# Three changes of order, and the second FFN matmul's right-hand loads issued by GpSimd, in a two-layer encoder kernel

## The chip, the cores and the metric

One core of a Trainium2 chip. The metric is the time of one execution in microseconds of device time (lower is better). Engines are named as in the profile: PE is TensorE, DVE is VectorE, ACT is ScalarE, POOL is GpSimd, and SP (SyncE) issues the transfers.

## The reference

A trunk of two encoder layers on x of 1024 tokens by 1024 features, all float32, conditioned by a vector c. Layer 0 mixes tokens with differential attention (8 heads, two score maps each), layer 1 with grouped-query attention (8 query heads, 2 key and value heads, RMS-normalised q and k, axial rotary). The feed-forward width is 2816.

```python
mod = (silu(c) @ ada_w[i] + ada_b[i])            # shift1, scale1, gate1, shift2, scale2, gate2
h = rmsnorm(x, norm1_g[i]) * (1.0 + scale1) + shift1
x = x + gate1 * mixer_i(h)                       # diff_attention or axial_gqa
h = rmsnorm(x, norm2_g[i]) * (1.0 + scale2) + shift2
gate, up = split(h @ w_in)
x = x + gate2 * ((silu(gate) * up) @ w_out)
...
return rmsnorm(x, final_g)
```

## The kernel before, in words

Activations are held transposed: 8 tiles `d` of 128 features, in two column chunks `c` of 512 tokens. Every float32 operand of a product is split into a high part (`whi`, a cast on ACT, L97) and a low part (`wlo`, a subtraction on DVE or POOL, L98), and one product becomes three matmuls: high times high (L107), high times low (L108), low times high (L109). One such "product of 128 by 512" is therefore three PE rows.

The framework orders each engine's instructions before the run, by the order in which they are written, by priorities, and by a simulated timeline. `issue_after(ins)` adds that an instruction comes behind `ins` on the same engine. Each engine then works its list in order, and so do the queues on which SP (and after the change POOL) issues transfers: a transfer that waits for its buffer holds up those behind it.

**Start (`start`, L344 to L420).** Row tiles of x are loaded (`load_x`, L360), eight of 128 by 1024. `scale` (L364) squares a tile on ACT, gets 1/rms by a power on POOL, and scales the tile in place (L372: chunk 0 on DVE, chunk 1 on POOL). `norm` (L374) transposes it on PE in blocks of 128 by 128 (L378), four to a bank, and ACT copies each bank out (L380). `mod(d)` (L382) loads two tiles of the modulation weights (L386), and DVE reduces them to the scale and shift of feature tile d (L387 to L390). `use(d, c)` (L393) makes the modulated h: the high part on ACT (L397), the same value on POOL (L398), the low part on DVE (L399); then come the products of tile d with the first head's q, k and v weights, 9 PE rows for each (d, c), 144 in all. The low parts of these three weights are made on POOL (`self.wlo`, L407).

**Layer 1, first projections (L684 to L709).** `steps` projects k, q or v of one head; a part is two of the eight feature tiles, so a projection of one chunk is four parts or 24 PE rows. `flush` (L622) finishes the k and q that are pending: a row sum on PE (L189), a power on POOL (L635), the rotary on DVE and POOL (L232 to L236), a broadcast of 1/rms on PE for k (L196) and its product on DVE (L643), then the split. Attention's first scores (L765 to L767) need k of both chunks.

**FFN input norm (`norm_parts`, L780).** For chunk 1, `step1` makes e, f and e - f for four pairs and writes the operands 7 and 3; `step2` subtracts three more times for each pair (`sub`, L797) and writes the operands 5, 6 and 4. The first products of chunk 1 (`plain(f, 1)`) take 3, 7, 7 and 3. All these subtractions and low parts are DVE's.

**Second FFN matmul (L1043 to L1166).** Seven products of blocks (a seven-product scheme in place of eight) in the order 1, 2, 6, 7, 5, 4, 3, each of 11 steps of 12 matmuls. A step needs one right-hand tile, loaded from the scratch `gd` into which the first matmul stored it (`right`, L1084; 77 loads a layer, 256 KB each, into `h` slots for products 1 and 2 and into eight `g` slots after that), and left-hand tiles of `w_out` (`left`, L1052; none to three a step, into five `raw` buffers and 22 `hb`). `ahead` writes a step's loads and splits LOOK = 4 steps ahead. At the end of products 2, 4, 5 and 3 POOL adds up squares for the next norm (`norm_acc`, L185).

Of the kernel before, what the change touches and what calls it, by code (L numbers as in the profile page):

```python
# [9 lines left out]
F32 = mybir.dt.float32  # L10
F32R = mybir.dt.float32r
AF = mybir.ActivationFunctionType
ALU = mybir.AluOpType
AX = mybir.AxisListType

P = 128
S = 1024
D = 1024
KT = 8
# [20 lines left out]
PARTS = 4  # L40
# [20 lines left out]
class Trunk:  # L61
# [33 lines left out]

    def split(self, hi, lo, src, eng=None):
        self.nc.scalar.copy(out=hi, in_=src)  # L97
        (eng or self.nc.vector).tensor_tensor(out=lo, in0=src, in1=hi.bitcast(F32), op=ALU.subtract)  # L98

    def mm3(self, ps, w, xs, n, w0=0, first=True, last=True, more=False):  # L100

# [242 lines left out]
    def start(self):  # L344

        nc, a = self.nc, self.a
        m, av = self.mods[0], self.avec[0][0]
        hs = [[None] * KT, [None] * KT]
        S0, S1 = self.t(self.pss, "S"), self.t(self.pss, "S")
        accs = [[S0[:, :CH], S0[:, CH:]], [S1[:, :CH], S1[:, CH:]], [self.bank("T"), self.bank("M")]]  # L350
        with self.tc.tile_pool(name="st", bufs=2) as st, self.tc.tile_pool(name="stx", bufs=8) as stx, \
                self.tc.tile_pool(name="stw", bufs=1) as stw, \
                self.tc.tile_pool(name="sta", bufs=4) as sta:
            xs = [[None] * KT, [None] * KT]

            def load_x(c):
                rows = []
                for i in range(4 * c, 4 * c + 4):
                    x = self.t(stx, "x0")
                    nc.sync.dma_start(out=x, in_=a["x"][i * P:(i + 1) * P, :])  # L360
                    rows.append(x)
                return rows

            def scale(c, rows):  # L364
                for x in rows:
                    sq = self.t(st, "sq")
                    r = self.t(st, "r0", [P, 2])
                    nc.scalar.activation(out=sq, in_=x, func=AF.Square, accum_out=r[:, 0:1])
                    nc.vector.tensor_scalar(out=r[:, 0:1], in0=r[:, 0:1], scalar1=1.0 / D, scalar2=EPS, op0=ALU.mult, op1=ALU.add)
                    nc.gpsimd.tensor_tensor(out=r[:, 1:2], in0=r[:, 0:1], in1=self.nhalf[:, :1], op=ALU.pow)  # L370
                    e = nc.vector if c == 0 else nc.gpsimd
                    e.tensor_scalar(out=x, in0=x, scalar1=r[:, 1:2], scalar2=0.0, op0=ALU.mult, op1=ALU.add)  # L372

            def norm(c, rows):  # L374
                for d in range(KT):
                    ps = self.bank("AT"[d % 2])
                    for i in range(4):
                        nc.tensor.transpose(ps[:, i * P:(i + 1) * P], rows[i][:, d * P:(d + 1) * P], self.ident)  # L378
                    xs[c][d] = self.hslot(F32)
                    nc.scalar.copy(out=xs[c][d], in_=ps)  # L380

            def mod(d):  # L382
                ds_ = slice(d, d + 1)
                for j in (1, 0):
                    w = self.t(sta, "aq")
                    nc.sync.dma_start(out=w, in_=a["ada_s"][j, d])  # L386
                    nc.vector.scalar_tensor_tensor(out=w, in0=w, scalar=1.0, in1=self.condr, op0=ALU.mult, op1=ALU.mult, accum_out=m[j][:, ds_])  # L387
                    b = C_ADAB + j * 8 + d
                    nc.vector.tensor_tensor(out=m[j][:, ds_], in0=m[j][:, ds_], in1=self.sm[:, b:b + 1], op=ALU.add)
                    if j == 1:  # L390
                        self.make_a(av[:, ds_], self.sm[:, C_N1 + d:C_N1 + d + 1], m[1][:, ds_])

            def use(d, c):  # L393
                sa, sb = av[:, d:d + 1], m[0][:, d:d + 1]
                hi, lo = hs[c][d] = self.hpair()
                h = self.t(st, "nh", [P, CH])
                nc.scalar.activation(out=hi, in_=xs[c][d], func=AF.Identity, bias=sb, scale=sa)  # L397
                nc.gpsimd.tensor_scalar(out=h, in0=xs[c][d], scalar1=sa, scalar2=sb, op0=ALU.mult, op1=ALU.add)  # L398
                nc.vector.tensor_tensor(out=lo, in0=h, in1=hi.bitcast(F32), op=ALU.subtract)  # L399
                for i in range(3):  # L400
                    self.mm3(accs[i][c], ws[i], hs[c][d:d + 1], 1, w0=d, first=d == 0, last=d == KT - 1)

            rows = [load_x(0), load_x(1)]
            self.condr = self.cond_row(self.cpool)
            mod(0)
            ws = []
            self.wlo = nc.gpsimd  # L407
            for i in range(3):
                raw = self.t(stw, "w0r") if i == 0 else None
                dst = (self.t(stw, "w0h", dt=F32R), self.t(stw, "w0l", dt=F32R)) if i == 0 else None  # L410
                ws.append(self.weights(a["wqkvA"][i], S, dst, raw))
            for c in range(2):
                scale(c, rows[c])
                norm(c, rows[c])
            for d in range(KT):
                if d:
                    mod(d)
                for c in range(2):
                    use(d, c)
        return hs, accs  # L420
# [184 lines left out]
    def layer1_attn(self, hs, norm, od, xsrc):  # L605
        nc, tc, a = self.nc, self.tc, self.a
        m = self.mods[1]
        with tc.tile_pool(name="b_tab", bufs=1, reuse_waits="tile") as tab, \
# [87 lines left out]
            for n in range(1, PARTS):  # L696
                first[1][n]()
                todo.pop(0)()
            for n in range(PARTS):
                first[2][n]()  # L700
                todo.pop(0)()
            flush()
            for s in todo:
                s()
            for s in first:
                for n in range(PARTS):
                    s[PARTS + n]()
            flush()
            vs[0] = self.v_natural(vp, vt[0])  # L709
            q = {h: steps(h, "q", h) for h in range(1, 8)}  # L710
            k1, v1 = steps(9, "k", 1), steps(11, "v", 1)
# [68 lines left out]
    def norm_parts(self, ft, bslot, tmp, xs, rb, av, bv, c, h0, ops):  # L780

        nc = self.nc
        t3 = {}

        def h_of(d, h):
            u = self.t(ft, "ft", [P, CH])
            h = u if h is None else h
            self.applied = nc.vector.scalar_tensor_tensor(out=u, in0=xs[d], scalar=av[:, d:d + 1], in1=rb, op0=ALU.mult, op1=ALU.mult)
            nc.scalar.activation(out=h, in_=u, func=AF.Identity, bias=bv[:, d:d + 1], scale=1.0)
            return h  # L790

        def put(i, f):
            hi, lo = bslot(), bslot()
            self.split(hi, lo, f)
            ops[i].append((hi, lo))

        def sub(o, x, y):  # L797
            nc.vector.tensor_tensor(out=o, in0=x, in1=y, op=ALU.subtract)

        def step0(d):  # L800
            h0[d] = h_of(d, bslot(F32))
            put(1 if d < 4 else 2, h0[d])

        def step1(d):
            e, f = h_of(d, None), h_of(d + 4, None)
            t = tmp()
            sub(t, e, f)
            put(7, t)
            put(3, f)
            t3[d] = t, e  # L810

        def step2(d):
            t, e = t3[d]
            sub(e, e, h0[d])
            put(5, e)
            sub(t, h0[d], t)
            put(6, t)
            sub(t, h0[d + 4], t)
            put(4, t)

        if c == 0:
            return [lambda d=d: step0(d) for d in (0, 4, 1, 5, 2, 6, 3, 7)]
        return [lambda d=d: step1(d) for d in range(4)] + [lambda d=d: step2(d) for d in range(4)]
# [43 lines left out]
    def ffn(self, layer, wo, xdst):  # L867
        nc, tc, a = self.nc, self.tc, self.a
        m = self.mods[layer]
        gate2 = m[5]  # L870
        with tc.tile_pool(name="hb", bufs=22, reuse_waits="tile") as hb, \
# [7 lines left out]
            xs = wo.xs  # L879
# [122 lines left out]
            start = plain(0, 0)  # L1002
# [78 lines left out]

            def right(i, k):
                t = self.hslot(F32) if i < 3 else g_tile()
                nc.sync.dma_start(out=t, in_=gd[i - 1, k])  # L1084
                hl = (self.t(hb, "hb", [P, CH], F32R), self.t(hb, "hb", [P, CH], F32R)) if i == 3 and k % 2 and not layer else self.hpair()
                with self.tc.high_priority(offset=WAHEAD):
                    self.split(*hl, t)
                return hl
# [23 lines left out]
            def norm(c, ps, spots=None, pool=None, tag="ft", between=None):  # L1112

                rb = self.norm_rb(box[c]["sq"], ps=ps, spots=spots, between=between)
                if layer == 0:
                    return self.norm_apply(pool or ft, xs[c], rb, self.avec[1][0], self.mods[1][0], hn[c], tag)
                return [lambda d=d: self.final(ft, xs[c], rb, d, 0, CH, c) for d in range(0, KT, 2)]
# [238 lines left out]
```

## Time and profile before

| | us |
|---|---|
| median of 3 runs (lowest, highest) | 2662.13 (2660.96, 2669.56) |
| the profiled execution's own time | 2666.48 |
| its span, first to last instruction | 2664.3 |
| PE busy in the span | 2531.1 (95%) |
| DVE busy | 1816.3 (68%) |
| ACT busy | 1250.8 (47%) |
| POOL busy | 927.2 (35%) |
| mean granted clock of TensorE | 0.978 |

A busy PE is one with a matmul in flight, at either of its clock levels (granted clock 1 is 2.4 GHz, 0.5 is 1.2 GHz). Idle time of an engine is put down to whatever released it. All 301 MB of transfers went through one queue, SP's.

### The profile page before, as it was taken

How to read it: one execution, taken by the hardware profiler on the slowest of the kernel's cores; microseconds unless marked ns; L12 is line 12 of the kernel's file. 1: busy time of each engine (PE TensorE's matmuls, PEld its weight loads, DVE VectorE, ACT ScalarE, POOL GpSimd, SP SyncE). 2: the span in 40 equal slices, each digit the busy share in tenths (PEclk: the TensorE clock that was granted, in tenths of full speed). 3: DMA queues.
4: the chain of work that ended last, by engine and by line, in shares of the span. 5: the costliest groups of instructions: out<-in, count | busy, mean ns of one | idle time of the engine just before them, and what ended most of it. 6: DMA issues, size and time to landing. Idle time of an engine off the chain costs nothing. (4 is left out here: it accounts for less than half of the span.)

```text
span 2664.3 us, 34917 instructions
## 1 busy us (share of the span) xinstructions
PE 2531.1 (95%) x12684; PEld 2073.6 (78%) x12684; DVE 1816.3 (68%) x2762; ACT 1250.8 (47%) x2175; POOL 927.2 (35%) x588
## 2 busy tenths in 40 slices
PE   6799999999998999999999899999999999999998
PEld 5577777777786878887787778888877888887787
DVE  6777778788757565556766677667657565656875
ACT  5555455555445434433534465656445333333542
POOL 7734545442133443330201366544133333330001
PEclk9899999999999999999999899999999999999999
DMA  7211111112213333338754222213122223228752
GB/s 263 72 48 52 64 48 60 56 64 92 72 52 109 113 126 131 131 111 302 237 162 151 85 88 79 92 45 119 56 71 91 95 107 107 104 99 316 225 180 81
DMA packets 145628, 303.44 MB, mean 114 GB/s; under 512 B 16048, under 2 KB 18352, under 8 KB 145456
## 3 DMA queue, kind: packets, MB, share of 16 engines
q1 hardware_dynamic: 145456, 301.21, 32.6%
q8 instruction: 100, 1.64, 0.2%
q14 instruction: 72, 0.59, 0.1%
HBM read 245.05 MB, written 56.10 MB: 113 GB/s over the span
## 5 line engine op out<-in xcount | busy, mean ns | idle before, releaser
L98 DVE TENSOR_TENSOR wlo<-raw,whi 128x512 fp32r<-128x512 f32 x400 | 316.9, 795 | 268.1 <-ACT whi L97 260.4
L97 ACT CAST whi<-raw 128x512 fp32r<-128x512 f32 x400 | 247.4, 620 | 512.4 <-PE S L108 307.3
L846 POOL TENSOR_TENSOR raw<-raw,raw 128x512 f32<-128x512 f32 x168 | 259.5, 1545 | 490.8 <-DVE wlo L98 271.4
L108 PE MATMUL S<-h,whi 128*128 128x512 f32 x984 | 390.0, 396 | 13.7 <-DVE h L98 13.6
L107 PE MATMUL S<-h,whi 128*128 128x512 f32 x984 | 389.7, 396 | 10.1 <-ACT whi L97 4.7
L109 PE MATMUL S<-h,wlo 128*128 128x512 f32 x984 | 387.8, 394 | 2.9 <-DVE wlo L98 2.9
L107 PE MATMUL M<-h,whi 128*128 128x512 f32 (+1 forms) x696 | 286.8, 412 | 15.9 <-ACT tmp L480 8.9
L109 PE MATMUL M<-h,wlo 128*128 128x512 f32 (+1 forms) x696 | 279.0, 401 | 1.6 <-POOL wlo L98 1.6
L108 PE MATMUL M<-h,whi 128*128 128x512 f32 (+1 forms) x696 | 277.8, 399 | 0.0
L108 PEld LDWEIGHTS S<-h,whi 128*128 128x128 f32 x984 | 187.1, 190 | 61.4 <-DVE h L98 23.1
L97 ACT CAST pt<-T 128x512 fp32r<-128x512 f32 x256 | 144.9, 588 | 189.6 <-PE T L267 188.2
L107 PEld LDWEIGHTS S<-h,whi 128*128 128x128 f32 x984 | 187.2, 190 | 56.6 <-ACT whi L97 6.4
L109 PEld LDWEIGHTS S<-h,wlo 128*128 128x128 f32 x984 | 187.2, 190 | 42.6 <-DVE wlo L98 4.2
L98 DVE TENSOR_TENSOR pt<-T,pt 128x512 fp32r<-128x512 f32 x256 | 171.1, 682 | 70.2 <-ACT pt L97 69.0
L185 POOL TENSOR_TENSOR ft<-ft,ft 128x512 f32<-128x512 f32 x43 | 72.0, 1674 | 381.3 <-ACT ft L181 380.0
L132 POOL TENSOR_TENSOR wraw<-wraw,cond 128x1024 f32<-128x1024 f32 x64 | 159.6, 2494 | 108.4 <-DMA wraw<-in_ada_t 96.5
L569 ACT ACTIVATE e<-S,mx 128x1024 f32<-128x1024 f32 x128 | 141.4, 1112 | 74.1 <-DVE mx L568 68.9
L107 PEld LDWEIGHTS M<-h,whi 128*128 128x128 f32 x696 | 134.5, 193 | 51.2 <-ACT tmp L480 12.4
L566 DVE TENSOR_REDUCE mx<-S 128x1 f32<-128x1024 f32 x128 | 150.1, 1213 | 33.8 <-PE S L558 33.7
L267 PE MATMUL T<-ident,e 128*128 128x128 f32 x1024 | 148.5, 279 | 16.1 <-DVE pt L98 12.8
L108 PE MATMUL S<-hb,whi 128*128 128x512 f32 x416 | 162.1, 390 | 1.7 <-DVE hb L98 1.7
L107 PE MATMUL S<-hb,whi 128*128 128x512 f32 x416 | 162.4, 390 | 1.0 <-ACT ft L970 1.0
(294 smaller groups left out, 5536.4 us busy)
## 6 DMA issues: line engine op xcount, KB each, us to landing
raw<-in_w_in SPq DMA_DIRECT2D x192, 256.0 KB, 2.7
gd<-g SPq DMA_DIRECT2D x154, 256.0 KB, 2.1
raw<-in_w_out SPq DMA_DIRECT2D x154, 256.0 KB, 3.4
wraw<-in_ada_t SPq DMA_DIRECT2D x64, 512.0 KB, 3.2
g<-gd SPq DMA_DIRECT2D x110, 256.0 KB, 3.7
wraw<-in_wqkvA SPq DMA_DIRECT2D x23, 512.0 KB, 3.2
h<-gd SPq DMA_DIRECT2D x44, 256.0 KB, 3.4
hb<-in_w_out SPq DMA_DIRECT2D x44, 256.0 KB, 5.2
```

The source lines that it names most:

```text
L97: self.nc.scalar.copy(out=hi, in_=src)
L98: (eng or self.nc.vector).tensor_tensor(out=lo, in0=src, in1=hi.bitcast(F32), op=ALU.subtract)
L107: mm(ps, lhsT=whi[:, ws], rhs=xh, start=first and k == 0 and not more, stop=False, skip_group_check=more)
L108: mm(ps, lhsT=whi[:, ws], rhs=xl, start=False, stop=False, skip_group_check=more)
L109: ins = mm(ps, lhsT=wlo[:, ws], rhs=xh, start=False, stop=last and k == n - 1, skip_group_check=more)
L132: nc.gpsimd.tensor_tensor(out=w, in0=w, in1=cond, op=ALU.mult)
L185: (eng or nc.gpsimd).tensor_tensor(out=box["sq"][:, ns], in0=box["sq"][:, ns], in1=sq[:, ns], op=ALU.add)
L267: nc.tensor.transpose(ps[:, i * P:(i + 1) * P], w[:, k * P:(k + 1) * P], self.ident)
L566: nc.vector.tensor_reduce(out=mx, in_=ps, op=ALU.max, axis=AX.X, negate=True)
L569: nc.scalar.activation(out=e, in_=ps, func=AF.Exp, bias=mx, scale=1.0, accum_out=sums[c])
L846: nc.gpsimd.tensor_tensor(out=o, in0=x, in1=y, op=op)
```

## The change

Four edits, of which the first three change orders (the first also moves work between engines), and the fourth the issuing engine of a transfer.

```diff
     def split(self, hi, lo, src, eng=None):
         self.nc.scalar.copy(out=hi, in_=src)
-        (eng or self.nc.vector).tensor_tensor(out=lo, in0=src, in1=hi.bitcast(F32), op=ALU.subtract)
+        return (eng or self.nc.vector).tensor_tensor(out=lo, in0=src, in1=hi.bitcast(F32), op=ALU.subtract)
...
-            def scale(c, rows):
+            def scale(rows):
+
+                diag = []
                 for x in rows:
...
-                    e = nc.vector if c == 0 else nc.gpsimd
-                    e.tensor_scalar(out=x, in0=x, scalar1=r[:, 1:2], scalar2=0.0, op0=ALU.mult, op1=ALU.add)
-
-            def norm(c, rows):
+                    dg = self.t(stx, "dg", [P, P])
+                    nc.vector.tensor_scalar(out=dg, in0=self.ident, scalar1=r[:, 1:2], scalar2=0.0, op0=ALU.mult, op1=ALU.add)
+                    diag.append(dg)
+                return diag
+
+            def norm(c, rows, diag):
...
-                        nc.tensor.transpose(ps[:, i * P:(i + 1) * P], rows[i][:, d * P:(d + 1) * P], self.ident)
+                        nc.tensor.matmul(ps[:, i * P:(i + 1) * P], lhsT=rows[i][:, d * P:(d + 1) * P], rhs=diag[i], start=True, stop=True)
...
-                nc.gpsimd.tensor_scalar(out=h, in0=xs[c][d], scalar1=sa, scalar2=sb, op0=ALU.mult, op1=ALU.add)
+                nc.scalar.activation(out=h, in_=xs[c][d], func=AF.Identity, bias=sb, scale=sa)
...
-            rows = [load_x(0), load_x(1)]
             self.condr = self.cond_row(self.cpool)
+            rows = [load_x(0)]
             mod(0)
             ws = []
-            self.wlo = nc.gpsimd
...
-            for c in range(2):
-                scale(c, rows[c])
-                norm(c, rows[c])
-            for d in range(KT):
-                if d:
-                    mod(d)
+            rows.append(load_x(1))
+            norm(0, rows[0], scale(rows[0]))
+            use(0, 0)
+            mod(1)
+            use(1, 0)
+            norm(1, rows[1], scale(rows[1]))
+            use(0, 1)
+            use(1, 1)
+            for d in range(2, KT):
+                mod(d)
                 for c in range(2):
                     use(d, c)
...
             for n in range(1, PARTS):
                 first[1][n]()
                 todo.pop(0)()
+            flush()
             for n in range(PARTS):
                 first[2][n]()
                 todo.pop(0)()
-            flush()
             for s in todo:
                 s()
-            for s in first:
+            for s in first[:2]:
                 for n in range(PARTS):
                     s[PARTS + n]()
             flush()
+            for n in range(PARTS):
+                first[2][PARTS + n]()
...
         def put(i, f):
             hi, lo = bslot(), bslot()
-            self.split(hi, lo, f)
+            t3["lo"] = self.split(hi, lo, f)
             ops[i].append((hi, lo))
+            if i == 3 and len(ops[3]) == 4:
+                t3["plain"] = t3["lo"]
 
         def sub(o, x, y):
-            nc.vector.tensor_tensor(out=o, in0=x, in1=y, op=ALU.subtract)
+            with self.tc.issue_after(t3["plain"].ins) if "plain" in t3 else contextlib.nullcontext():
+                nc.vector.tensor_tensor(out=o, in0=x, in1=y, op=ALU.subtract)
...
             def right(i, k):
                 t = self.hslot(F32) if i < 3 else g_tile()
-                nc.sync.dma_start(out=t, in_=gd[i - 1, k])
+                nc.gpsimd.dma_start(out=t, in_=gd[i - 1, k])
```

## Rows read from the trace of the kernel before

**Rows 1.** The page, busy time and share of PE and POOL.

```profile
PE 2531.1 (95%) x12684; PEld 2073.6 (78%) x12684; DVE 1816.3 (68%) x2762; ACT 1250.8 (47%) x2175; POOL 927.2 (35%) x588
```

**Rows 2.** Busy us by stretch: PE, PEld, DVE, ACT, POOL; granted clock, DMA share, GB/s.

```profile
0.00:72.00 72.00, 51.03 (x212) 37.96 (x212) 48.12 (x98) 40.39 (x64) 50.06 (x40) 0.93 0.65 244
...
793.00:843.00 50.00, 44.85 (x184) 35.42 (x184) 41.63 (x61) 27.91 (x48) 17.90 (x8) 0.90 0.25 85
...
1228.00:1320.00 92.00, 84.66 (x350) 66.32 (x349) 64.91 (x103) 38.71 (x69) 8.33 (x2) 0.96 0.83 286
...
1498.00:1580.00 82.00, 70.76 (x364) 57.75 (x365) 56.60 (x81) 48.18 (x83) 48.90 (x27) 0.92 0.28 100
...
1991.00:2046.00 55.00, 49.80 (x208) 39.29 (x208) 44.57 (x67) 28.70 (x50) 18.37 (x8) 0.91 0.21 72
...
2430.00:2510.00 80.00, 75.19 (x309) 57.95 (x308) 59.78 (x91) 35.41 (x63) 4.27 (x3) 0.98 0.77 257
```

**Rows 3.** The same view, the first 20 us.

```profile
0.00:20.00 20.00, 8.58 (x35) 5.88 (x35) 5.68 (x19) 14.65 (x26) 10.00 (x18) 1.00 0.91 356
```

**Rows 4.** Timeline of PE, first and last of the start's 144 products.

```profile
28.59 0.80 PE L107 MATMUL S<-h,w0h 128*128 128x512 f32 x1 [1.87 <-ACT h L397]
...
71.11 0.39 PE L108 MATMUL M<-h,whi 128*128 128x512 f32 x1
71.33 0.40 PE L109 MATMUL M<-h,wlo 128*128 128x512 f32 x1
```

**Rows 5.** Groups of instructions, 0 to 72 us: DVE, POOL and ACT in turn.

```profile
L387 DVE SCALAR_TENSOR_TENSOR aq<-aq,cond 128x1024 f32<-128x1024 f32 x16 | 24.7, 1547 | 1.9 <-DMA aq<-in_ada_s 1.1 <-ACT cond L121 0.8
...
L398 POOL TENSOR_SCALAR nh<-h,a,mod 128x512 f32<-128x512 f32 x16 | 28.5, 1786 | 7.6 <-DVE mod L389 5.0 <-DVE a L173 2.7
...
L397 ACT ACTIVATE h<-h,mod,a 128x512 fp32r<-128x512 f32 x16 | 12.3, 809 | 22.8 <-DVE mod L389 17.2 <-DVE a L173 5.6
```

**Rows 6.** Timeline of PE: four float32 products of 128 by 128 at full clock.

```profile
1476.64 1.05 PE L196 MATMUL A<-ident,r 128*128 128x128 f32 x8
```

**Rows 7.** Timelines of PE, then POOL, 1509 to 1526 us: layer 1's second flush.

```profile
1509.95 0.95 PE L189 MATMUL M<-ones,tmp 128*128 128x1 f32 x8
...
1514.58 2.07 PE L196 MATMUL M<-ident,kr 128*128 128x128 f32 x8 [2.42 <-POOL kr L635]
...
1525.16 0.62 PE L765 MATMUL S<-h,h 128*128 128x512 f32 x2
...
1512.44 2.08 POOL L635 TENSOR_TENSOR kr<-qss,nhalf 128x8 f32<-128x8 f32 x1
```

**Rows 8.** Timelines of PE, DVE and ACT, 2008 to 2022 us: layer 1's FFN input norm.

```profile
2015.39 0.80 PE L108 MATMUL S<-h,whi 128*128 128x512 f32 x1 [2.04 <-DVE h L98]
2017.80 0.80 PE L108 MATMUL S<-h,whi 128*128 128x512 f32 x1 [0.76 <-DVE h L98]
2021.76 0.80 PE L108 MATMUL S<-h,whi 128*128 128x512 f32 x1 [2.31 <-DVE h L98]
...
2008.63 0.68 DVE L798 TENSOR_TENSOR ft<-ft,h 128x512 f32<-128x512 f32 x1
...
2019.36 1.75 DVE L798 TENSOR_TENSOR g<-h,g 128x512 f32<-128x512 f32 x1
2021.03 0.68 DVE L98 TENSOR_TENSOR h<-ft,h 128x512 fp32r<-128x512 f32 x1
...
2020.59 0.62 ACT L97 CAST whi<-raw 128x512 fp32r<-128x512 f32 x1 [6.17 <-POOL raw L846]
```

**Rows 9.** Who waited for whom, 1210 to 1320 us: PE, then SP's queue.

```profile
PE T L107 <- ACT h L97: 2.3, 2, 1.3
...
SPq L1084 <- DVE h L98: 8.4, 17, 2.0
```

**Rows 10.** POOL's adds in layer 0's second FFN matmul: min/median/max ns.

```profile
L185 POOL TENSOR_TENSOR ft<-ft,ft x7: 1285/1617/14630, 1311.1 to 1430.7; 128x512 f32<-128x512 f32 x7
```

**Rows 11.** The page, DMA issues: right-hand loads, KB each, median us to landing.

```profile
g<-gd SPq DMA_DIRECT2D x110, 256.0 KB, 3.7
```

## The prediction

> **What bounds the kernel now.** I read the page first: PE is busy for 2531.1 of 2664.3 us [rows 1], so 133 us of idle time, and whatever runs at the lower clock, is all that an order can win back. The profiled execution's own time is 2666.48 us, 4.35 above the median of 2662.13; I make the sum against the profiled one and carry the difference over to the median.
>
> Then the busy time by stretch shows where the 133 us lie as far as this change touches them [rows 2]. The start (0 to 72 us) has PE busy for 51.0, so 21 us idle, at a mean clock of 0.93. The two FFN input norms (793 to 843 and 1991 to 2046) have 5.2 us idle each, with DVE busy for 41.6 of 50 and 44.6 of 55. The turn from projections to attention in layer 1 (1498 to 1580) has 11.2 us idle at a clock of 0.92. The beginnings of the two second FFN matmuls (1228 to 1320 and 2430 to 2510) have 7.3 and 4.8 us idle, while the transfers take 83% and 77% of the DMA engines. That is 55 us in all, the ceiling but for the clock. Last, timelines and waits of these stretches show which wait ends last in each.
>
> **The start.** What moves: x's chunk 1 goes behind the weights of the first head. Before, twelve loads of 512 KB stand ahead of what the first product needs (eight of x, the condition row, two modulation tiles, a weight); afterwards eight do. The first 20 us move 356 GB/s [rows 3], so four loads (2.1 MB) are 5.9 us, and the first product, at 28.59 us now [rows 4], can come at some 22 us or earlier. But only tile 0 of chunk 0 (9 PE rows) can run then; the next needs chunk 1 of x or the second pair of modulation tiles, which stand behind x's chunk 1. The last x tile is fourteenth in the queue: 7.3 MB at 356 GB/s is 20.6 us, with a square, a power and the landing some 26 us.
>
> What is added: the 64 transposes become 64 float32 products with a diagonal. Four such 128 by 128 products take 1.05 us at full clock [rows 6] and 2.07 us where PE had stood idle [rows 7]. So chunk 1's 32 cost between 8.4 and 16.6 us, and now they lie between the products instead of ahead of them; chunk 0's fall into time in which PE waits for weights. From 26 us PE has 8.4 us of these and 135 products at a spacing of 0.23 us [rows 4], 31 us: 65.4 us, against the end at 71.7 us now.
>
> The rest of this edit: POOL gives up 16 passes at 1786 ns, and ACT takes 16 at 809 ns [rows 5], 13 us on an engine with 31 us free in these 72 [rows 2]. DVE takes three weight splits of twice 0.68 us [rows 8] and eight diagonals, which I bound by 0.68 us each, 7.5 us at most; it loses four scalings, and its 16 reductions of 1547 ns [rows 5] no longer run beside POOL's passes. I cost both at nothing: DVE has 24 us free in the stretch [rows 2]. If that cover is gone, DVE sets the end, by at most these 7.5 us. I take a **gain of 6**. Bounds: a gain of 16 if the 5.9 us come and every stall between the products goes (43.1 us from first to last less 144 times 0.23 us is 10), a loss of 7 if all of chunk 1's diagonal products run at 2.07 us a group and 5 us more of the products at the lower clock.
>
> **The flush in layer 1.** Now the row sum of q's second chunk stands behind all of v (1509.95 us), the power behind it takes 2.08 us, PE stands for 2.42 us waiting for it, and the broadcast then runs at 2.07 instead of 1.05 us [rows 6, 7]. Only 10 us later do the scores of the second key half start, at 1525.16. Afterwards 24 PE rows of v (5.5 us at 0.23) lie behind the flush and cover the power: 2.42 + 1.02, and something for products at the lower clock behind that wait: **gain of 4**. The first flush moves ahead of v's first chunk as well, so its rotary comes ahead of some of the norm's tiles on DVE; DVE's sum is the same. Bounds: a loss of 2.4 if the norm's last tile comes later by as much as that wait, a gain of 8 (most of the 11.2 us idle) if the first softmaxes hide behind v.
>
> **The FFN input norm.** PE stands for 2.04 + 0.76 + 2.31 = 5.1 us, three times for a low part of DVE [rows 8]. Six of the twelve `step2` subtractions were put ahead of the low part that ends the last of these (starts from 2008.63 to 2019.36, five at a spacing near 0.6 us, one of 1.75, about 4.7 us). The edit puts all twelve behind it; nothing waits in a queue that was not in DVE's already, and their own low parts are wanted by products some 22 us later (96 PE rows). So up to 4.7 us a layer. What is late next: ACT's cast of a later weight waits until 2020.59 for a POOL sum [rows 8], and PE, 4.7 us earlier, would reach that weight some 1.2 us too soon. I take 3.5 a layer, **gain of 7**; bounds 0 and 10.2. Layer 0 has the same idle time within 0.1 us [rows 2].
>
> **The right-hand loads.** 154 loads leave SP's queue and join POOL's. What SP gains: in the first stage it stood for 8.4 us, 17 times, until a right-hand buffer came free [rows 9], with `w_out` loads behind. What PE waits for there is, in one group of 2.3 us, the cast of a right-hand tile [rows 9]. Upper bound: all the idle time of the two beginnings, 7.3 + 4.8 = 12. What POOL's queue does to the loads: a load has five steps of 12 matmuls, 13.8 us, less 3.7 us of landing [rows 11] and 1.3 us for cast and low part, so 8.8 us of slack. The trace has no transfer issued by POOL. The nearest row is POOL's own add beside a busy DVE: 1285 ns at best, 14630 at worst [rows 10]. A burst of such adds, 15.9 us, ahead of a load overdraws the slack by 7.1 us; one burst in each layer makes the lower bound, a loss of 14. Between ends so alike I take **0**, nearer the median add (1617 ns), which overdraws nothing. The Trainium skill ("DMA: Bandwidth & Descriptors", section "Issuing engines are not separate DMA queues") holds that transfers of different issuers share the same DMA engines, and a second issuer saves only issue time. By it this term is also about 0; by the row on SP's waits up to 12 are there, since what SP loses is waiting behind a buffer, not issue time.
>
> **Sum.** 6 + 4 + 7 + 0 = 17: 2649.5 for the execution profiled, 2645 for the median. A measurement of this kernel can tell about 0.3%, 8 us, from no change: faster begins below 2654, slower above 2670.
>
> **Rivals.**
>
> *Loads stuck behind POOL's adds* (slower). POOL works in order; there are six bursts of adds in the two second matmuls. If each runs like the longest, PE stalls six times for 7.1 us, 43 us: 2645 + 43 = 2688. It decides from the third burst on (21 against 17), and shows beyond the noise with four. For: the add of 14630 ns, in a stretch where DVE is busy for 65 of 92 us [rows 2, 10]. Against: the median add is 1617 ns, and most of the 77 loads of a layer have no add near them. The Trainium skill ("SBUF — State Buffer", "Who interferes with whom") says that DVE shuts GpSimd out wholly in its two-port modes, also from writing descriptors, but that a tensor_tensor with two SBUF inputs hinders only GpSimd's reads. DVE's low parts are tensor_tensor, so by the page the descriptors pass and only the adds are slow; no row here shows a descriptor being written.
>
> *The start pays nothing, or the subtractions alone pay.* If the diagonal products eat up the earlier loads and the simulated timeline puts the flush where it was (the change then doesn't do what it says there), 7 us stay: 2655, within the noise. For: 8.4 to 16.6 us of new PE work against 5.9 us of earlier data. Against: PE is idle for 21 us in that stretch.
>
> *All four pay in full*: 12 + 7 + 9 + 10 = 38, 2624. For: the waits are measured, and waits that go take half-clock stretches with them. Against: the transfers are near their limit where the last 10 should come from, and a weight is late next in the norm.
>
> **How the numbers follow.** The forecast and its surroundings (2637 to 2653) get 0.50, all in full 0.21, little 0.18, POOL's queue 0.11. The range of 8 in 10 runs from 2624 to 2662: it leaves out the slow rival and the deepest part of the full one. Faster is the forecast and the full case with 0.01 of the little one: 0.72. Within 0.3% lie the rest of the little case and 0.02 of POOL's queue, 0.19. Slower is 0.09.
>
> **What would show it.** Right: the first product near 20 us, the start's last one near 65; no PE wait for POOL's power near 1500, and the first score of the second key half some 10 us sooner behind the last projection; the three stalls in each FFN input norm gone or one short one left, with a cast or a weight's low part as releaser; PE gapless in the later steps of the second FFN matmul as now. Wrong: the last product of the start at 72 or later; PE waits for a cast of g or h in the middle of the second FFN matmul, at the places of POOL's adds; a busy POOL in that stage with loads that land later than 8.8 us behind their turn.

## The result, and the profile after

The changed kernel takes 2680.1 us (median; 2677.7 to 2686.8), the kernel before 2662.1 in the same comparison: a ratio of 1.0072, 95% interval 1.0058 to 1.0087. It is 18 us slower, where the prediction had 17 us faster and a range of 2624 to 2662.

The page of the changed kernel: span, the busy line that answers to [rows 1], the queues by kind, and the DMA issues that answer to [rows 11] (median us to landing last).

```profile
span 2681.0 us, 35116 instructions
...
PE 2536.8 (95%) x12748; PEld 2082.8 (78%) x12748; DVE 1813.8 (68%) x2769; ACT 1260.6 (47%) x2191; POOL 952.3 (36%) x719
...
q0 software_dynamic: 12320, 40.38, 4.6%
...
g<-gd POOLq DMA_DIRECT2D x110, 256.0 KB, 4.2
...
h<-gd POOLq DMA_DIRECT2D x44, 256.0 KB, 6.3
```

The loads did move: 154 of them, 40.38 MB, are now a queue of their own. PE is busy for only 6 us more (64 matmuls more, and products at the lower clock); the other 11 of the 17 us by which the span grew are idle time. Busy time by stretch, the changed kernel's answer to [rows 2], with the same columns:

```profile
0.00:72.00 72.00, 53.16 (x276) 43.78 (x276) 43.02 (x107) 52.31 (x81) 10.79 (x17) 1.00 0.65 244
793.00:843.00 50.00, 44.66 (x190) 35.61 (x189) 45.67 (x66) 29.66 (x51) 14.74 (x7) 0.97 0.29 102
1228.00:1320.00 92.00, 80.54 (x324) 62.20 (x323) 61.92 (x93) 35.72 (x64) 20.75 (x34) 0.94 0.70 243
1498.00:1580.00 82.00, 72.63 (x380) 60.44 (x379) 54.63 (x80) 46.39 (x80) 46.82 (x27) 0.94 0.28 99
1991.00:2046.00 55.00, 49.74 (x214) 39.67 (x215) 46.03 (x69) 30.18 (x53) 14.92 (x8) 0.97 0.23 80
2430.00:2510.00 80.00, 64.34 (x240) 48.67 (x239) 45.79 (x72) 22.82 (x41) 11.22 (x21) 0.89 0.62 213
```

The two beginnings of the second FFN matmul lose 4.1 and 10.9 us of busy PE against before, and the clock falls with it (0.98 to 0.89 in the last). In layer 0 the changed kernel comes to that stage 8.6 us sooner, so the first of these two windows catches less of the loss. The four other stretches lie within 2.2 us of before. What PE waits for in the second of the two beginnings: timeline of PE in the changed kernel, 2436 to 2475 us, the rows with idle time ahead of them.

```profile
2444.98 0.51 PE L107 MATMUL T<-h,whi 128*128 128x512 f32 x1 [1.00 <-ACT h L97]
2448.63 0.80 PE L108 MATMUL T<-h,whi 128*128 128x512 f32 x1 [3.15 <-DVE h L98]
2454.49 0.49 PE L107 MATMUL T<-h,whi 128*128 128x512 f32 x1 [0.96 <-ACT h L97]
2456.78 0.79 PE L108 MATMUL T<-h,whi 128*128 128x512 f32 x1 [1.79 <-DVE h L98]
2462.83 0.50 PE L108 MATMUL T<-h,whi 128*128 128x512 f32 x1 [1.51 <-DVE h L98]
2467.82 0.50 PE L108 MATMUL T<-h,whi 128*128 128x512 f32 x1 [1.97 <-DVE h L98]
2474.45 0.80 PE L108 MATMUL S<-h,whi 128*128 128x512 f32 x1 [3.62 <-DVE h L98]
```

Five of the seven waits, 12 of 14 us, are for the low part (L98) of a right-hand tile: four of product 1 (bank T), the last of product 2 (S). The other two, of 1 us each, are for a high part (L97). And here is VectorE (DVE) in the same stretch. L1089 is the running sum of product 2 over two `w_out` tiles (L1077 before), L1070 the difference for product 6; neither is wanted yet.

```profile
2447.89 0.68 DVE L98 TENSOR_TENSOR h<-h,h 128x512 fp32r<-128x512 f32 x1
2450.27 0.69 DVE L1089 TENSOR_TENSOR hb<-hb,raw 128x512 f32<-128x512 f32 x1 [1.70 <-DMA raw<-in_w_out]
...
2454.22 0.69 DVE L1089 TENSOR_TENSOR hb<-hb,raw 128x512 f32<-128x512 f32 x1 [2.53 <-DMA raw<-in_w_out]
...
2456.04 0.68 DVE L98 TENSOR_TENSOR h<-h,h 128x512 fp32r<-128x512 f32 x1
2460.76 0.69 DVE L1089 TENSOR_TENSOR hb<-hb,raw 128x512 f32<-128x512 f32 x1 [4.04 <-DMA raw<-in_w_out]
2461.48 0.69 DVE L1070 TENSOR_TENSOR hb<-hb,hb 128x512 f32<-128x512 f32 x1
2462.09 0.68 DVE L98 TENSOR_TENSOR h<-h,h 128x512 fp32r<-128x512 f32 x1
```

VectorE stands for a `w_out` tile (4.04 us ahead of 2460.76), with the low part that PE wants behind it. PE goes on at 2448.63, 2456.78 and 2462.83, each time less than a microsecond after the low part began. Why the `w_out` tiles are late, from the DMA issues of 2430 to 2460 us, first before, then after:

```profile
raw<-in_w_out SPq DMA_DIRECT2D x17, 256.0 KB, 4.0
h<-gd SPq DMA_DIRECT2D x5, 256.0 KB, 3.8
```

```profile
raw<-in_w_out SPq DMA_DIRECT2D x13, 256.0 KB, 6.3
h<-gd POOLq DMA_DIRECT2D x13, 256.0 KB, 7.1
```

In SP's one queue five `h` loads stood among 17 `w_out` loads. On a queue of their own 13 are issued in the same 30 us, ahead of need, and the `w_out` loads into `raw` fall to 13 and land in 6.3 us instead of 4.0. In layer 0 the same change is smaller: 17 and 15 loads, landing in 5.1 us before and 6.2 after (1238 to 1268 and 1230 to 1260 us). That left three suspects: the loads' order on GpSimd (the first eight loads for product 6 stand ahead of the last three for product 1 and of all for product 2, and one of the eight waited 19.28 us for a buffer), the running ahead, and the order of VectorE's list.

### The profile page after: what moved, and what is told of

It is laid out like the page before. It is cut to its first block, busy times and chain, and to the rows that moved or that the text cites. A ratio compares the mean times of both kernels' runs of the same rounds, so it can differ in the third digit from the quotient of the medians.

```text
span 2681.0 us, 35116 instructions
## 1 busy us (share of the span) xinstructions
PE 2536.8 (95%) x12748; PEld 2082.8 (78%) x12748; DVE 1813.8 (68%) x2769; ACT 1260.6 (47%) x2191; POOL 952.3 (36%) x719
## 3 DMA queue, kind: packets, MB, share of 16 engines
q0 software_dynamic: 12320, 40.38, 4.6%
## 4 chain that ended last, share of the span: by engine, by line
PE 65%; DVE 13%; DMA 7%; issue 6%; ACT 6%; POOL 3%; POOLq 0%; DVEq 0%; ACTq 0%
PE S L108 10%; PE S L107 10%; PE S L109 10%; PE M L107 5%; PE M L108 4%; PE M L109 4%; DMA raw<-in_w_out 4%; PE A L279 3%; PE T L107 3%; PE T L109 3%; PE T L108 3%; PE T L267 3%; DVE h L98 2%; PE S L565 2%; PE A L281 2%
## 5 line engine op out<-in xcount | busy, mean ns | idle before, releaser
L97 ACT CAST whi<-raw 128x512 fp32r<-128x512 f32 x400 | 247.7, 620 | 588.4 <-PE S L108 351.9
L98 DVE TENSOR_TENSOR wlo<-raw,whi 128x512 fp32r<-128x512 f32 x400 | 320.0, 802 | 259.0 <-ACT whi L97 255.2
L97 ACT CAST pt<-T 128x512 fp32r<-128x512 f32 x256 | 145.2, 587 | 175.4 <-PE T L267 174.2
L98 DVE TENSOR_TENSOR pt<-T,pt 128x512 fp32r<-128x512 f32 x256 | 171.2, 682 | 72.8 <-ACT pt L97 72.4
L107 PEld LDWEIGHTS M<-h,whi 128*128 128x128 f32 x696 | 133.6, 192 | 47.9 <-ACT tmp L487 12.2
L109 PE MATMUL S<-hb,wlo 128*128 128x512 f32 x416 | 161.9, 389 | 0.0
```

Of the source, the lines that this page charges most:

```text
L98: return (eng or self.nc.vector).tensor_tensor(out=lo, in0=src, in1=hi.bitcast(F32), op=ALU.subtract)
L107: mm(ps, lhsT=whi[:, ws], rhs=xh, start=first and k == 0 and not more, stop=False, skip_group_check=more)
L109: ins = mm(ps, lhsT=wlo[:, ws], rhs=xh, start=False, stop=last and k == n - 1, skip_group_check=more)
```

## The experiments

Ratios are to the kernel before, run beside each experiment on the same chip; medians in us compare less well, since the kernel before has 2662 on one chip and 2667 to 2669 on others. Stages are read from first and last instructions: *p1* is from product 5's last sum in the first FFN matmul to the first sum of product 1's result in the second (the stretch in which most of the loss sits), *rest* from there to the last such sum, *turn* from layer 0's last sum to layer 1's first softmax. One profile each, layer 0 / layer 1, in us:

| kernel | ratio, 95% interval | p1 | rest | turn |
|---|---|---|---|---|
| before | 1 | 30.2 / 32.1 | 193.9 / 178.3 | 66.5 |
| after | 1.0072 (1.0058 to 1.0087) | 41.4 / 45.7 | 191.3 / 182.9 | 68.6 |
| e1 orders alone | 1.0008 (0.9996 to 1.0019) | 30.4 / 32.8 | 197.8 / 180.8 | 68.0 |
| e2 loads alone | 1.0099 (1.0080 to 1.0117) | 42.0 / 44.6 | 191.4 / 180.5 | 65.3 |
| e6 loads in program order | 1.0092 (1.0074 to 1.0110) | 36.7 / 37.8 | 197.4 / 184.1 | 64.7 |
| e9 44 early loads | 1.0084 (1.0068 to 1.0101) | 44.6 / 42.7 | 191.2 / 178.7 | 65.4 |
| e8 110 late loads | 1.0043 (1.0028 to 1.0058) | 31.2 / 32.1 | 197.7 / 179.3 | 66.5 |
| e10 e9, paced | 1.0148 (1.0130 to 1.0166) | 36.9 / 35.1 | 198.4 / 185.1 | 63.9 |
| e11 e9, sums later | 1.0007 (0.9994 to 1.0019) | 37.5 / 34.6 | 191.0 / 177.0 | 65.7 |
| e12 before, sums later | 0.9973 (0.9961 to 0.9985) | 28.8 / 30.8 | 192.1 / 177.1 | 65.2 |
| e16 e2, sums later | 1.0005 (0.9987 to 1.0023) | 31.7 / 34.6 | 191.1 / 179.1 | 63.8 |
| e13 after, sums later | 0.9988 (0.9975 to 1.0002) | 32.2 / 34.4 | 190.6 / 178.7 | 70.0 |
| e3 norm edge alone | 0.9964 (0.9951 to 0.9977) | 30.2 / 32.5 | 193.0 / 178.2 | 63.9 |
| e4 start alone | 1.0004 (0.9989 to 1.0019) | 30.6 / 32.3 | 198.0 / 178.0 | 65.3 |
| e5 flush alone | 1.0027 (1.0013 to 1.0041) | 31.1 / 32.1 | 194.4 / 178.5 | 70.2 |
| e15 flush held ahead | 0.9999 (0.9987 to 1.0011) | 30.5 / 32.1 | 192.4 / 178.7 | 65.0 |
| e14 e3 and e12 | 0.9944 (0.9925 to 0.9964) | 28.4 / 30.1 | 192.0 / 177.3 | 66.5 |
| e17 e14 and start | 0.9941 (0.9920 to 0.9962) | 29.3 / 30.1 | 191.2 / 176.3 | 63.9 |

Two cautions on these stretches. p1 begins with a sum on VectorE, and how far PE is by then differs: 110 and 128 PE rows start in the two p1 stretches before, 131 in each of e2's, so that some 5 of the 24 us between them are the marker's. And long stretches differ from one execution to the next: ten kernels that are the same up to 1200 us have product 5's last sum in layer 0 anywhere from 1228.7 to 1245.2 us, while rest of layer 0 is 192.4 to 194.4 us in the four kernels that leave that stage and the start alone (before, e3, e5, e15).

**Which part loses.** e1 is the changed kernel with one line put back, e2 the kernel before with that line alone:

```
- e1:   nc.gpsimd.dma_start(out=t, in_=gd[i - 1, k])
+ e1:   nc.sync.dma_start(out=t, in_=gd[i - 1, k])
```

> The changed kernel with its right-hand loads back in SP's queue: the three orders alone. Theory (the loads cost all of the loss): between the markers of the two traces the second FFN matmul lost about 6 us in layer 0 and 19.5 in layer 1, 25 together, so without the loads the changed kernel stands at 2680 less 25, about 2655 (2650 to 2659), below the kernel before. Rival (the orders rearrange the engines so that the second matmul loses by itself): 2670 or more, with the stalls at its beginning still there.

> The kernel before with the right-hand loads issued by GpSimd and nothing else. Theory (the loads cost all of the loss): 2662 plus 25, about 2687 (2680 to 2693), above the changed kernel. Rival (the orders lose, the loads are harmless, as the prediction had it): 2662 within 4.

The loads cost 1.0099, 26 us, by themselves, so they are the loss. The two p1 stretches are 11.8 and 12.5 us longer, some 19 us in all without the marker's share: 10 are idle time of PE, and 8 to 9 are the clock's by an estimate from the granted clock (0.88 and 0.89, against 0.96 and 0.99 before). But the orders alone gain nothing (1.0008), where 2655 was expected: in e1 `rest` takes 4 us longer in layer 0 and 2.5 in layer 1. What the stages ahead of it win can't be read from one profile: product 5's last sum in layer 0 comes at 1227.8 us instead of 1236.1, 1 us ahead of the range given above. So the theory held for e2 and failed for e1. Nor do the parts add up: with the loads on GpSimd the orders are worth some 7 us (1.0072 against 1.0099), with the loads on SP nothing.

**The order on GpSimd's queue.** e6 chains the 154 loads in program order; e9 gives GpSimd only the 44 loads of products 1 and 2, so that no later load can stand among them:

```
+ e6:   with self.tc.issue_after(rl[0].ins) if rl else contextlib.nullcontext():
+           rl[:] = [nc.gpsimd.dma_start(out=t, in_=gd[i - 1, k])]
+ e9:   (nc.gpsimd if i < 3 else nc.sync).dma_start(out=t, in_=gd[i - 1, k])
```

> The kernel before with GpSimd issuing the right-hand loads, but each held in the program's order behind the one before it, so that no load for the third product stands ahead of one for the second. Theory (the wrong order of GpSimd's list is what costs): the loss goes, 2658 to 2666. Rival 1 (a queue of their own lets these loads run ahead of need and take the DMA engines from the left-hand loads, in whatever order): 2675 to 2690, with w_out landings of 6 us or more near 2440. Rival 2 (a load issued by GpSimd costs more as such, every one): 2680 or more, with the stalls spread over the whole of the second matmul.

> The kernel before with only the 44 right-hand loads of the first two products issued by GpSimd, the 110 of the five later ones by SP. Theory (wrong order, later loads ahead of earlier ones in one list): that order cannot arise, 2658 to 2666. Rival 1 (running ahead): the loss stays, 2675 to 2690. Rival 2 (a cost per load): 44 of 154 of a loss of 25, about 2669.

1.0092 and 1.0084: the order on the queue is not what the loss hangs on, and 44 of the 154 loads make 22 of the 26 us. That also speaks against a price per load. Yet the order isn't without effect. In e6 the `w_out` loads into `raw` land in 4.5 us (2447 to 2477 us), where the first rival had 6 or more, and the two p1 stretches are 12 us shorter than e2's together; but `rest` is 10 us longer. The order moves the loss and doesn't take it away.

> The kernel before with only the 110 right-hand loads of the five later products issued by GpSimd; the 44 of the first two stay in SP's queue. Theory (what costs is that the first two products' loads no longer stand among the w_out loads in one queue; an issue by GpSimd as such costs nothing): 2658 to 2666. Rival (each load that GpSimd issues costs more): 110 of 154 of 27.8, about 2682. Between the two, near 2672: the eight loads of the third product that stand at the beginning run ahead too.

e8 is e9's line turned round (`nc.sync if i < 3`). Its p1 stretches are those of before, as the theory has it, yet it is 11.5 us slower, some 5 of them in the two `rest` stretches. Its profile doesn't place the others: product 5's last sum in layer 0 comes 9 us later than before, at 1245.2 us, but up to there VectorE's and ACT's lists are those of before.

**Pacing, or VectorE's list.** Two ways to part the suspects that were left. e10 holds each early load behind a copy of one column, on GpSimd, of the `w_out` tile two steps back. e11 lets the loads run ahead as in e9 and only puts each running sum behind a low part that is wanted sooner:

```
+ e10:  rl[:] = [nc.gpsimd.tensor_copy(out=self.pace[:, 0:1], in_=raws[-2][:, 0:1])]
...
- e11:  later[i, k] = lambda: tt(out=s1[k], in0=s1[k], in1=u, op=ALU.add)
+ e11:  def later_add():
+           with self.tc.issue_after(lows[k + 8].ins):
+               tt(out=s1[k], in0=s1[k], in1=u, op=ALU.add)
```

`lows[n]` is the low part of the n-th right-hand tile; the sum of product 2's tile k belongs to step 11 + k.

> As e9 (44 early loads by GpSimd), but each load waits behind a one-column copy on GpSimd of the w_out tile of two steps earlier, so that it can't run ahead of the left-hand loads. Theory (running ahead takes the DMA engines from w_out): the loss of 24 goes, 2658 to 2668, and w_out lands in some 4 us near 2445. Rival (the issue by GpSimd costs, or the order of VectorE's list): 2680 or more.

> As e9, with the loads still running ahead, but each running sum of VectorE on the second product's w_out tiles (the operation that waits for a late w_out tile) held behind the low part of the right-hand tile that is wanted three or more steps sooner. Theory (late w_out tiles alone cost): little changes, 2678 to 2686, PE then waits for the weights. Rival (the loads change the order of VectorE's list: low parts of tiles that have landed stand behind sums that wait): most of the 24 goes, 2660 to 2670.

e10 doesn't part the two. It is slower by 39 us, and GpSimd stands for 43.2 us in 13 waits for `w_out` tiles (2415 to 2500 us); but PE waits for only 5.4 us there, and most of the 39 us lie elsewhere. The products of both FFNs stand 233 ns apart instead of 227, 2.5% more, also where no moved load is near. A stretch in which PE has no gap and the full clock, before and then e10 (columns as in [rows 2]), and e10's page, which answers to [rows 1]:

```profile
1000.00:1100.00 100.00, 100.00 (x446) 82.72 (x445) 58.80 (x76) 40.81 (x71) 36.98 (x27) 1.00 0.38 132
```

```profile
1000.00:1100.00 100.00, 100.00 (x435) 80.72 (x434) 57.69 (x75) 40.59 (x71) 36.60 (x27) 1.00 0.39 130
...
PE 2566.0 (95%) x12684; PEld 2077.8 (77%) x12684; DVE 1818.6 (67%) x2762; ACT 1251.2 (46%) x2175; POOL 950.9 (35%) x672
```

The same 12684 matmuls keep PE busy for 34.9 us more. What in the edit does that, no run shows; besides the copies it adds a tile of 128 by 2. Some 4 or 5 us are left for the pacing (an estimate, 39 less 34.9), against 22 in e9, so the loss has largely gone in e10. But both suspects changed in it. Fewer early loads run ahead: 30 us behind product 5's last sum 15 of a layer's 22 are issued, where e9 has issued 20 and the kernel before 12, and the `w_out` loads into `raw` land in 5.3 us (2458 to 2488), against 6.6 in e9 (2430 to 2460). And on VectorE the tenth right-hand low part stands behind two running sums, as before, where it stands behind five in e9.

e11 is clear: 1.0007 instead of 1.0084, with the loads as far ahead as in e9 (20 of 22) and `raw` tiles that land in 6.3 us (2433 to 2463). Its control, and the same edge with all 154 loads on GpSimd, without and with the orders:

> The kernel before, all loads in SP's queue, with the same edge as in e11 (running sums behind low parts). Theory (e11's edge puts right what the loads had put wrong, and before it was right): within 4 of before. Rival (the edge gains 24 of its own, beside a loss that stays): some 24 below before.

> The kernel before with all 154 right-hand loads by GpSimd and the edge of e11 on the running sums, no orders. Theory (of the loss of 28, the order of VectorE's list is 20 or more): 2662 to 2670; from product 5 to the end of product 1 some 33 us a layer, against 42 to 45 without the edge and 30 to 32 before. Rival (late w_out tiles are the larger part): 2675 or more.

> The changed kernel, all 154 loads by GpSimd, with the edge of e11. Theory (the order of VectorE's list is the cause in the changed kernel too, and what is left is the orders' gain): the loss of 17 goes and some of the gain ahead of the second matmul shows, 2650 to 2662. Rival (with all loads on GpSimd the wrong order there or the late tiles still cost): 2670 or more.

e16 stands at 1.0005 where e2 has 1.0099; the two differ in that edge alone. Who waited for whom, VectorE and then PE, e2 from 2440 to 2520 us, then e16 from 2430 to 2510 (total us, times, longest):

```profile
DVE hb L1077 <- DMA raw<-in_w_out: 15.0, 8, 3.5
...
PE S L108 <- DVE h L98: 6.3, 6, 3.6
PE T L108 <- DVE h L98: 5.9, 3, 3.0
PE T L107 <- ACT h L97: 2.0, 2, 1.0
```

```profile
DVE wlo L98 <- ACT whi L97: 13.2, 10, 3.3
...
PE T L107 <- ACT h L97: 3.6, 2, 2.6
PE S L108 <- DVE h L98: 3.5, 4, 1.3
PE T L108 <- DVE h L98: 0.5, 2, 0.3
```

And the landings of `w_out`, e2 from 2440 to 2470 us, e16 from 2430 to 2460:

```profile
raw<-in_w_out SPq DMA_DIRECT2D x14, 256.0 KB, 5.8
h<-gd POOLq DMA_DIRECT2D x13, 256.0 KB, 6.8
```

```profile
h<-gd POOLq DMA_DIRECT2D x15, 256.0 KB, 6.3
raw<-in_w_out SPq DMA_DIRECT2D x14, 256.0 KB, 5.8
```

The tiles land as late in e16 as in e2 (5.8 us, 14 of them), and the loads run ahead as far; but VectorE's 15.0 us of waiting in front of the low parts has gone, and PE's waits for low parts fall from 12.2 to 4.0 us. So late tiles cost little as such; they cost because VectorE's list has sums that wait for them ahead of low parts whose tiles are there. The control says how much of the edge's worth is that repair: with the loads on SP it gains 0.27%, 7 us, too, where the theory had expected nothing. The kernel before has the same fault in small: sums that wait stand ahead of low parts in its list as well, though in layer 1 VectorE stands at them for only 1.1 us (2427 to 2507 us), which alone isn't the 7. If gain and repair add up, some 7 of the 25 us between e2 and e16 are the edge's own gain, and 18 the repair; 8 or 9 us of the loads' cost stay under it (1.0005 against 0.9973).

**The three orders one by one.**

> The kernel before with only the edge in the FFN input norm (the subtractions behind the last low part of the third operand). The prediction: 3.5 a layer, 2655 (2652 to 2662). By the markers of the changed kernel, 3.5 in layer 1 and nothing in layer 0: 2658.5.

> The kernel before with only the new order of the start. The prediction: a gain of 6 (between 16 and a loss of 7), 2656. By the marker at the end of the start in the changed kernel: a gain of 1, 2661. Rival (the rest of the program is drawn up otherwise by the planner because of it, and loses): 2665 or more, with the end of the start no later than before.

> The kernel before with only the moved flush in layer 1. The prediction: a gain of 4 (between 8 and a loss of 2.4), 2658. Rival (the norm's last tiles come later by as much): 2662 to 2666, with the first softmax of layer 1 no sooner after the last sum of layer 0.

0.9964, 1.0004 and 1.0027, together 0.9995: the orders add up to nothing, as e1 says. The flush loses. e5's PE around the second flush, and its wait, which answer to [rows 7]:

```profile
1511.48 1.05 PE L189 MATMUL M<-ones,tmp 128*128 128x1 f32 x8
...
1517.72 0.95 PE L189 MATMUL M<-ones,tmp 128*128 128x1 f32 x8
...
1523.20 1.83 PE L196 MATMUL M<-ident,kr 128*128 128x128 f32 x8 [1.91 <-POOL kr L635]
```

The first row sum (of k) stands at 1511.48, the second (of q) at 1517.72, with 20 of the 24 PE rows of v's second chunk between them: the kernel's text puts them behind the flush, PE's list does not. So the wait for the power stays, and the first softmax comes 3.7 us later (turn): 70.2 us, where the kernels whose order there is that of before have 63.8 to 66.5. e15 moves that flush alone and holds the chunk behind the row sum on PE:

```
+ for s in first[:2]: ...second chunk...
  flush()
+ with tc.issue_after(self.sums.ins):
+     for n in range(PARTS):
+         first[2][PARTS + n]()
```

> The kernel before with the second flush of layer 1 alone moved ahead of v's second chunk, and that chunk held on PE behind the flush's last row sum; the first flush stays where it was. Theory (the loss of 7 in e5 came from the row sum's staying behind v and from the first flush): no wait of PE for the power near 1515, the first softmax of layer 1 up to 4 us sooner behind layer 0's last sum than before (66.5 us), 2656 to 2662. Rival (a flush ahead of v costs by itself): 2666 or more, 68 us or more.

In e15 the row sums come at 1502.67 and 1505.82 and the broadcast runs without a wait and at full clock:

```profile
1505.82 1.70 PE L189 MATMUL M<-ones,tmp 128*128 128x1 f32 x8
...
1514.50 1.06 PE L196 MATMUL M<-ident,kr 128*128 128x128 f32 x8
```

The stage takes 65.0 us, inside the range of the kernels that leave the flush alone, and the program is the same (0.9999). The longest wait of PE in e15 from 1498 to 1545 us:

```profile
PE T L267 <- DVE pt L98: 4.0, 1, 4.0
```

What is late next is a softmax's low part, for which PE waited 0.4 us before.

**The best version.** e14 is the kernel before with the edges of e3 and e12, loads in SP's queue; e17 adds the start.

> The kernel before, loads in SP's queue, with the edge in the FFN input norm (e3) and the edge on the running sums (e12), nothing else. If the two add up: 0.36% and 0.27% below before, 2662 less 17, 2645 (2641 to 2651). If one redraws what the other gained: 2653 to 2658.

> As e14, with the new order of the start as well. Theory (the start's gain of 1 to 2 us is lost because layer 0's second matmul is drawn up anew, 198 instead of 194 us; the edge on the sums pins that): at most 1 to 2 us below e14, with 192 us in that stage. Rival (the start gives nothing in any case): at e14 or up to 4 above it.

e14 beats both kernels: 0.9944, 15 us below before, 1.3% below the changed one. The start adds nothing that can be told (0.9941).

## Why the prediction was wrong

**The right-hand loads** were the step that failed: "Between ends so alike I take 0" for a term that measures a loss of 26, outside the bounds of 12 and -14. Not the size but the place was wrong. The working asked whether a right-hand load comes in time, and gave it 8.8 us of slack; they came early, and the tiles that came late were left-hand ones. SP's single queue had paced the right-hand loads (5 issued near 2440 us where GpSimd issues 13), and the prediction counted the waits in it as something to win ([rows 9], 8.4 us) instead of asking what they held back. And it looked at GpSimd's queue for what stands behind a wait, not at VectorE's list, which decides what a late tile costs: with the low parts ahead of the sums 25 of the 26 us go (e16), some 18 of them as the repair of what the loads did.

The Trainium skill ("DMA: Bandwidth & Descriptors", section "Issuing engines are not separate DMA queues"), which the prediction weighed as "about 0", says that transfers of different issuers interleave on the same DMA engines. The traces agree (`w_out` landings go from 4.0 to 6.3 us near 2440 us, and from 5.1 to 6.2 in layer 0, once GpSimd issues beside SP); what the prediction read out of it, that nothing is lost, doesn't follow.

The slower rival gave 2688 for its own reason, loads stuck behind GpSimd's adds. That reason falls: e16 has the same 154 loads in the same queue as the adds, and stands at 1.0005; its `rest` stretches, in which the adds lie, take 370.2 us together, against 369.2 with the loads on SP (e12).

**The start**: a gain of 6 predicted, between -5 and +3 us measured (e4). In the changed kernel the first product is at 25.18 instead of 28.59, where "some 22 us or earlier" was said; the last is at 70.36 instead of 71.33 [rows 4]. The step that failed is the 31 us for 135 products without a gap from 26 us on. They run without a gap only from 41.39 us on, and by then 126 of the 144 are still to come, 29 us at 0.23 (timeline of PE in the changed kernel):

```profile
25.18 0.50 PE L107 MATMUL S<-h,w0h 128*128 128x512 f32 x1
...
41.39 0.50 PE L107 MATMUL S<-h,w0h 128*128 128x512 f32 x1 [1.39 <-ACT h L401]
...
70.36 0.39 PE L109 MATMUL M<-h,wlo 128*128 128x512 f32 x1
```

Until then PE has 18 of them beside the diagonal products, and from 20 us on it stands for ACT's copies of the banks (2.9 us), the modulated h (1.6), a diagonal (1.2) and a low part (1.1). VectorE, whose work the prediction covered with 24 us of free time, has none just there (e4, columns as in [rows 2]); over the whole stage it is busy for 43.0 us against 48.1 before, although its new work was put too low (4.1 for the splits and 5.4 for the diagonals are 9.5 us, not 7.5).

```profile
30.00:40.00 10.00, 8.46 (x57) 7.12 (x57) 9.93 (x23) 7.03 (x13) 2.52 (x1) 1.00 0.76 253
```

The microsecond won is lost again in layer 0's second matmul (198.0 against 193.9 us), which the start doesn't touch. e1 has nearly the same, 197.8; e17, with the sums' edge, 191.2. In e4 and e1 ACT's and VectorE's lists have another order in that stage than before; that this is the cause is not shown, and e8 has 197.7 without the new start.

**The flush**: a gain of 4 predicted, a loss of 7 measured (3 to 11). "24 PE rows of v (5.5 us at 0.23) lie behind the flush and cover the power" is the step that failed: they didn't, as the rival had it that "the simulated timeline puts the flush where it was". Where e15 makes them lie there, the wait goes as predicted, and a wait that the sum hadn't named takes most of its place.

**The FFN norm**: a gain of 7 predicted, 9.6 measured (6 to 13), the one term whose number held. Its mechanism held in part. In each layer PE's waits for low parts fall from 5.1 [rows 8] to 2.6 us, from three to one long one and one of 0.2 us, so half of these waits stays, where one short wait at most was forecast; the other half of the gain comes with the clock, which the sum had left out. The 30 us from the first gated product of layer 1, before and then e3 (columns as in [rows 2]):

```profile
2007.40:2037.40 30.00, 24.88 (x93) 18.70 (x93) 28.59 (x44) 16.55 (x31) 11.54 (x3) 0.83 0.27 92
```

```profile
2007.50:2037.50 30.00, 27.36 (x112) 21.59 (x111) 27.24 (x41) 15.38 (x29) 11.56 (x6) 0.94 0.31 101
```

PE does 19 matmuls more in this time, 4.4 us at 0.23 each: 2.5 us less idle time and a clock of 0.94 instead of 0.83. Layer 0 has the same (111 instead of 92). In layer 0 (who PE waited for, 793 to 843 us, the changed kernel) the weight's cast is late next, as the prediction feared: 2.7 us, once, beside 2.6 us of low parts.

```profile
PE T L107 <- ACT whi L97: 2.7, 1, 2.7
PE S L108 <- DVE h L98: 2.6, 2, 2.4
```

From the first gated product to product 5's last sum, the six kernels with this edge take 425.7 us on average in layer 0 and 416.2 in layer 1, eleven without it (e10 left out) 430.0 and 420.3: 8 of the 9.6 us, the same in both layers.

**What stays open**: the 8 or 9 us that loads on GpSimd still cost under the edge, e8's 11.5 us, the wider spacing of e10's products, and whether late tiles with VectorE's list of before would have cost as much as with the new one. From the eighth on, most low parts stand one to three sums later in the changed kernel's list than before (the tenth behind five sums instead of two), and no run had the late tiles with the list of before.

## What to carry to other kernels

A wait in a shared in-order queue may be what paces its loads: before a kind of load is moved to a queue of its own, ask what it will overtake, and which engine waits for the loads that are overtaken. Where an engine's list is drawn up by a planner, look for operations that wait on far data and stand ahead of operations whose data is there; one ordering edge was worth 7 us in the kernel before and 22 in the changed one. Where a variant is slower, look first whether work that its edit doesn't touch still takes its old time (e10). And a reordering is worth what the lists say after it, so read there whether the moved step moved, and what waits next.

## What the hardware showed unexpectedly

A 256 KB load occupies GpSimd for 546 ns at its issue and SP's queue for 320 (`g`) or 384 ns (`h`), all medians; with 154 of them beside VectorE's `tensor_tensor` operations none took over 747 ns. The changed kernel's loads by their line, ns min/median/max, first and last start:

```profile
L1096 POOL DMA_DIRECT2D g<-gd x110: 536/546/566, 1215.2 to 2597.3; - x110
L1096 POOL DMA_DIRECT2D h<-gd x44: 536/546/747, 1199.7 to 2465.7; - x44
```

With loads outstanding on two queues both kinds land later: near 2440 us `w_out` went from 4.0 to 6.3 us and `h` from 3.8 to 7.1, both 256 KB, while the DMA engines were full (2430 to 2460 us: SP's queue 54.3% of them, GpSimd's 45.8%). The Trainium skill ("DMA: Bandwidth & Descriptors", section "SWDGE vs HWDGE vs iDMA") says that each DMA engine takes the queues of the two kinds in turn; that agrees with these landings, though no run here shows a single engine's turns.
